# Float32 products for the last rows of gate and up weights in a mixture-of-experts trunk

## The chip, the cores and the metric

The kernel runs on one core of a Trainium2 chip. The metric is the device time of one execution in microseconds (us). Before the change it is 1541.08 us, the median of three runs (1535.46 to 1543.49).

## The reference

The reference is a trunk of two decoder layers over 256 tokens of width 1024, all in float32. Each layer projects the tokens, runs differential attention (4 heads) and a gated delta rule (4 heads) side by side, projects back, and normalises. The first layer then has a dense SwiGLU, the second a mixture of 8 experts of which each token takes 2:

```python
def swiglu(x, w_gate, w_up, w_down):
    return (jax.nn.silu(x @ w_gate) * (x @ w_up)) @ w_down
...
logits = jnp.einsum('td,de->te', xf, router_w).astype(jnp.float32)
top_val, top_idx = lax.top_k(logits, TOP_K)
gates = jax.nn.softmax(top_val, axis=-1)
...
y = swiglu(xb, w_gate[e_b], w_up[e_b], w_down[e_b])
out = jax.ops.segment_sum(y * w_buf[:, None], tok_buf, num_segments=T)
```

An expert has a gate and an up matrix of 1024 x 3584 and a down matrix of 3584 x 1024. The weights of the eight experts are 352 MB, read once. They take about 960 of the 1544 us; this is the part that the change touches, together with the first loads of the kernel.

## The kernel before, in words

**Precision.** TensorE multiplies a reduced float32 type (float32r) here. A weight piece `raw` is therefore split in two: ScalarE writes `wh`, the piece rounded to float32r (line 173), and VectorE writes `wl = raw - wh` (line 176). The activations are split the same way into a high and a low part, and the product is made of xh·wh, xl·wh and xh·wl.

**Experts.** Expert 0 comes first, then the other seven, which the kernel orders by how many tokens they drew. The three with the fewest tokens are *narrow*: they have 64 token slots. The other five are *wide*, with 128. The order is wide, narrow, wide, narrow, wide, narrow, wide, wide. An expert's hidden width is cut in two chunks of 1792 columns, numbered c = 0 and 1. For each chunk the kernel streams, in this order:

1. the gate weights in 8 pieces (k = 0 to 7) of 128 x 1792, each one DMA of 896 KB, each cut into two halves of 896 columns that are split into `wh` and `wl`; the products go to four banks of PSUM, two named `mm` and two named `gd`, 448 columns each;
2. three pieces of the down weights of the chunk before (`more()`, two rows of blocks of 1024 columns, 1 MB, two halves); the silu of the gate (`hh`, line 1165) is between the first and the second of them;
3. the up weights in 8 pieces, into four fresh banks with the same names;
4. the four pieces of down weights that remain; behind the first of them VectorE multiplies silu and up (`hh`, line 1185).

The products of a half in a wide expert are 4 with `wh` and 2 with `wl`. In a narrow expert the high and the low part of the 64 tokens lie beside each other in one stationary operand of 128 columns, so a half needs 2 products with `wh` and 2 with `wl`, and the results of the low part come out in rows 64 to 127 of the bank. At the end of a stream `leads` copies these rows to a tile `room` on ScalarE (line 1101), and four more products with a shift matrix (`moves`) add them to rows 0 to 63. `leads` is called behind the eighth piece, ahead of the first down piece; the moves come behind that down piece. `room` has two buffers, so the third and the fourth copy wait for the first two moves.

**What sets the order.** Each engine runs its instructions in an order that is fixed when the kernel is compiled. A planner makes it from the order in which the code names the instructions and from its own estimates of when each is ready; it may put an instruction ahead of an earlier one. `pin(...)` holds an instruction behind the one that was named before it on its engine, while later ones may still pass it. The copies of `leads`, the silus and the multiplications are pinned. Loads of weights are pinned on the queue of SyncE (SP), each waiting until its buffer is free: 12 buffers for raw pieces, four each for `wh` and `wl`. A buffer of a raw piece is free when VectorE has made `wl` from it.

**Start.** SP issues the positions (`pos_i`), the first constants (`cst0`), the first 128 tokens, two weight pieces of 520 KB, the other 128 tokens, two more pieces, and then the rest. Meanwhile POOL issues nine small loads, most of which broadcast a row to 128 partitions: the parameters of the delta rule (`al`), of two norms (`nrm`), of lambda (`prow`) and the router's weights (`rw`).

Of the kernel before, what the change touches and what calls it, by code (L numbers as in the profile page):

```python
# [9 lines left out]
F32 = mybir.dt.float32  # L10
# [7 lines left out]
P = 128  # L18
# [49 lines left out]
def trunk(ctx, tc, x, positions, w_in, conv_w, a_log, dt_bias, gdn_norm_w, lam_q1, lam_k1, lam_q2, lam_k2,  # L68
# [13 lines left out]
    def nm(s):  # L82
        cnt[0] += 1
        return f"{s}_{cnt[0]}"
# [118 lines left out]

    zab0 = []
    pos_i = pre.tile([P, NB], I32, name="pos_i")
    nc.sync.dma_start(pos_i, positions.rearrange("o (b p) -> p (o b)", p=P))
    nc.sync.dma_start(cst0, const[:, :P + 32])
# [768 lines left out]
    def experts(xs, jobs, mp, ring2, rest, first):  # L976
# [22 lines left out]
        def dispatch(group, early=False):  # L999
# [20 lines left out]

            return xgs, [lambda k=k: part(k) for k in range(KD)]

        def transposed(n):
            Dt = mp.tile([P, NB, P], F32R, tag="ys", name=nm("D"))
            slots(Dt, jobs[n], True)
            DT = mp.tile([P, NB, P], F32R, tag=f"DT{n % 2}", name=nm("DT"), bufs=1)
            pt = bank("a")
            for b in range(NB):
                PE.transpose(pt[:, b * P:(b + 1) * P], Dt[:, b].bitcast(F32), ident)
            V.tensor_copy(DT.rearrange("p b t -> p (b t)"), pt[:, 0:NB * P])  # L1030
            return DT

        def in_pieces(w, c, k0=0):

            for k in range(k0, KD):
                yield k, piece(w[:, k:k + 1, c * CHUNK:(c + 1) * CHUNK], 1, CHUNK)

        def products(outs, xg, narrow, k, parts):
# [56 lines left out]
        def leads(banks):  # L1095

            hi = slice(64, P)
            moves = []
            for p in banks:
                o = mp.tile([P, BANK], F32R, tag="room", name=nm("room"), bufs=2)  # L1100
                pin(S.activation(o[hi], p[hi, :], AF.Copy))
                moves.append(lambda o=o, p=p: mm(p[0:64, :], shift[hi, 0:64], o[hi], False, True))
            return moves

        def to_features(hh, narrow):
# [29 lines left out]
        for n, job in enumerate(jobs):  # L1135
            narrow = job[3]
            rows = slice(0, 64) if narrow else slice(0, P)
            xg = xgs.pop(n)
            wg, wu = (weights(n, i).rearrange("(k p) c -> p k c", p=P) for i in range(2))
            for c in range(NC):  # L1140
                banks = gu_banks()
                for k, f in enumerate(first or ()):
                    products(banks, xg, narrow, k, f)
                for sub in in_pieces(wg, c, len(first or ())):
                    products(banks, xg, narrow, *sub)
                    if side:
                        side.pop(0)()
                first = None
# [24 lines left out]
                for sub in in_pieces(wu, c):  # L1173
                    products(banks, xg, narrow, *sub)
# [4 lines left out]
                moves = leads(banks) if narrow else ()  # L1179
                more()  # L1180
                for move in moves:
                    move()
                for i, p in enumerate(banks):
                    h = hh[rows, i * BANK:(i + 1) * BANK]
                    pin(V.tensor_tensor(h, h, p[rows, :], op=ALU.mult))  # L1185
# [150 lines left out]
    nc.gpsimd.dma_start(al[:, 1], dt_bias.partition_broadcast(P))  # L1336
    nrm = pre.tile([P, 2, 2, P], F32, name="nrm")
    nc.gpsimd.dma_start(nrm[:, 0], subln_w.partition_broadcast(P))
    nc.gpsimd.dma_start(nrm[:, 1], gdn_norm_w.partition_broadcast(P))
    prow = pre.tile([P, 2 * 4 * 64], F32, name="prow")  # L1340
    for i, a in enumerate((lam_q1, lam_k1, lam_q2, lam_k2)):
        nc.gpsimd.dma_start(prow[:, i * 128:(i + 1) * 128], a.rearrange("l d -> (l d)").partition_broadcast(P))


    cw = pre.tile([P, 12, 8], F32, name="cw")


    rw = cpool.tile([P, KD, NE], F32, name="rw")
    nc.gpsimd.dma_start(rw, router_w[0].rearrange("(k p) e -> p k e", p=P))
# [72 lines left out]
```

## Time and profile before

| What | Value |
|---|---|
| median of three runs | 1541.08 us (1535.46 to 1543.49) |
| the profiled execution, its own time | 1546.4 us |
| its span on the core | 1544.4 us |
| instructions | 24332 |
| read from memory | 431.17 MB, 280 GB/s over the span |
| granted TensorE clock, mean | 0.973 of 2.4 GHz |

The span is what the profiler recorded on the core; the execution's own time is 2.0 us longer. The trace names engines PE (TensorE products), PEld (its weight loads), DVE (VectorE), ACT (ScalarE), POOL (GpSimd) and SP (SyncE's queue). A tile stands as out<-in. Products of TensorE overlap each other in the records, so their starts tell their pace, not their durations. The idle time of an engine before an instruction stands in brackets with what ended it.

### The profile page before, as it was taken

To read this page: it belongs to the slowest core of one execution; us is meant where nothing else is said; L and a number is where in the kernel's file an instruction comes from. 1 tells how busy PE (TensorE), PEld (TensorE's weight loads), DVE (VectorE), ACT (ScalarE), POOL (GpSimd) and SP (SyncE) were. 2 spreads that over 40 slices of the span, in tenths; PEclk is the share of its full clock that TensorE was granted. 3 is DMA by queue.
4 is the path that set the end of the run, shared out by engine and by line. 5 is a ranking of instruction groups with operands and counts; after the bars stand their busy time and mean duration, and the time that the engine had idled before them with its cause. 6 is when DMAs were issued, how large, how long until landed. Compare 5 with 4: busy or idle time off the path is not lost. (4 is left out here: it accounts for less than half of the span.)

```text
span 1544.4 us, 24332 instructions
## 1 busy us (share of the span) xinstructions
PE 1471.1 (95%) x8864; PEld 1239.8 (80%) x8864; DVE 1253.9 (81%) x1630; ACT 1092.3 (71%) x1577; POOL 23.6 (2%) x36
## 2 busy tenths in 40 slices
PE   7989999999999999999999999899999899999996
PEld 7968899998978888866787876688876677898884
DVE  5787655556796789888899888889889989988996
ACT  3747544456657388887787797887887878778774
POOL 1000000000000000000000000000000000000000
PEclk8999999999999799999999999999999999999998
DMA  9523465545533589999999999999999999999870
GB/s 315 208 83 110 154 203 190 191 138 188 172 109 114 191 313 367 337 394 326 366 398 330 375 358 326 379 368 351 381 339 373 330 365 400 342 356 361 306 299 31
DMA packets 89127, 433.95 MB, mean 281 GB/s; under 512 B 7816, under 2 KB 9992, under 8 KB 74912
## 3 DMA queue, kind: packets, MB, share of 16 engines
q1 hardware_dynamic: 87808, 428.54, 75.2%
q0 software_dynamic: 1184, 3.71, 0.9%
q8 instruction: 73, 1.20, 0.3%
q14 instruction: 62, 0.51, 0.1%
HBM read 431.17 MB, written 1.05 MB: 280 GB/s over the span
## 5 line engine op out<-in xcount | busy, mean ns | idle before, releaser
L176 DVE TENSOR_TENSOR wl<-raw,wh 128x896 fp32r<-128x896 f32 (+2 forms) x875 | 962.1, 1142 | 192.5 <-ACT wh L173 175.0
L173 ACT ACTIVATE wh<-raw 128x896 fp32r<-128x896 f32 (+2 forms) x875 | 844.9, 995 | 242.2 <-PE ps_gd L101 89.5
L101 PE MATMUL ps_b<-wh,hT 128*128 128x512 f32 x816 | 239.1, 405 | 7.6 <-ACT wh L173 6.0
L101 PE MATMUL ps_gd<-wh,xg 128*128 128x448 f32 x832 | 223.7, 367 | 0.0
L101 PE MATMUL ps_mm<-wh,xg 128*128 128x448 f32 x832 | 218.8, 371 | 1.0 <-ACT hh L1165 1.0
L101 PEld LDWEIGHTS ps_b<-wh,hT 128*128 128x128 f32 x816 | 155.5, 193 | 49.8 <-ACT wh L173 14.0
L101 PE MATMUL ps_b<-wl,hT 128*128 128x512 f32 x492 | 168.8, 424 | 11.2 <-DVE wl L176 11.1
L101 PEld LDWEIGHTS ps_gd<-wh,xg 128*128 128x128 f32 x832 | 156.4, 188 | 13.9
L101 PEld LDWEIGHTS ps_mm<-wh,xg 128*128 128x128 f32 x832 | 152.6, 189 | 15.3 <-ACT hh L1165 1.3
L101 PE MATMUL ps_gd<-wl,xg 128*128 128x448 f32 x512 | 153.5, 380 | 4.8 <-DVE wl L176 1.2
L101 PE MATMUL ps_mm<-wl,xg 128*128 128x448 f32 x512 | 151.1, 373 | 3.3 <-DVE wl L176 3.0
L101 PEld LDWEIGHTS ps_b<-wl,hT 128*128 128x128 f32 x492 | 91.8, 198 | 52.5 <-DVE wl L176 30.9
L101 PEld LDWEIGHTS ps_gd<-wl,xg 128*128 128x128 f32 x512 | 90.3, 188 | 34.3 <-DVE wl L176 26.1
L101 PEld LDWEIGHTS ps_mm<-wl,xg 128*128 128x128 f32 x512 | 93.3, 188 | 20.0 <-DVE wl L176 12.1
L101 PE MATMUL ps_mm<-xT,wh 128*128 128x256 f32 x448 | 70.9, 280 | 0.0
L101 PEld LDWEIGHTS ps_mm<-xT,wh 128*128 128x128 f32 x448 | 60.8, 189 | 0.4
L101 PE MATMUL ps_gd<-xT,wh 128*128 128x256 f32 x320 | 50.5, 280 | 0.0
L101 PE MATMUL ps_mm<-xT,wl 128*128 128x256 f32 x224 | 44.7, 280 | 0.0
L1119 ACT ACTIVATE hT<-ps_a 128x512 fp32r<-128x512 f32 (+2 forms) x52 | 27.5, 540 | 22.1 <-PE ps_a L1117 15.2
L101 PEld LDWEIGHTS ps_gd<-xT,wh 128*128 128x128 f32 x320 | 43.1, 189 | 0.0
L1117 PEld LDWEIGHTS ps_a<-cst,hh 128*128 128x128 f32 (+1 forms) x224 | 32.2, 201 | 6.9 <-DVE hh L1185 4.1
L1120 DVE TENSOR_TENSOR hT<-ps_a,hT 128x512 fp32r<-128x512 f32 (+2 forms) x52 | 31.8, 619 | 7.0 <-ACT hT L1119 6.9
(401 smaller groups left out, 1591.1 us busy)
## 6 DMA issues: line engine op xcount, KB each, us to landing
raw<-in_moe_w_gate_dram SPq DMA_DIRECT2D x128, 896.0 KB, 7.3
raw<-in_moe_w_up_dram SPq DMA_DIRECT2D x128, 896.0 KB, 6.5
raw<-in_moe_w_down_dram SPq DMA_DIRECT2D x110, 1024.0 KB, 6.8
raw<-in_w_in_dram SPq DMA_DIRECT2D x24, 1024.0 KB, 6.0
raw<-in_ffn_w_gate_dram SPq DMA_DIRECT2D x11, 1024.0 KB, 5.2
raw<-in_ffn_w_up_dram SPq DMA_DIRECT2D x11, 1024.0 KB, 5.1
raw<-in_ffn_w_down_dram SPq DMA_DIRECT2D x11, 1024.0 KB, 4.9
raw<-in_w_out_dram SPq DMA_DIRECT2D x8, 1024.0 KB, 4.9
```

The lines of the kernel that those rows point to most:

```text
L101: return PE.matmul(o, lhsT, rhs, start=start, stop=stop, skip_group_check=True)
L173: high = S.activation(wh[:, c:c + n], w, AF.Copy)
L176: low = V.tensor_tensor(wl[:, c:c + n], w, wh[:, c:c + n].bitcast(F32), op=ALU.subtract)
L1117: PE.transpose(pt[:, f * w:(f + 1) * w], hv[:, f0 + f], ident[rows, rows])
L1119: S.activation(hT[:, f0:f0 + n_, 0], pv, AF.Copy)
L1120: V.tensor_tensor(hT[:, f0:f0 + n_, 1], pv, hT[:, f0:f0 + n_, 0].bitcast(F32), op=ALU.subtract)
```

## The change

There are four edits.

- In a narrow expert the eighth piece (k = 7) of gate and up is loaded but not split. VectorE adds the high and the low part of the tokens once per expert into a float32 tile `x32` of 64 columns (`as_one`), and TensorE multiplies it by the raw piece in float32: four products of 448 columns in place of eight in float32r. They write rows 0 to 63.
- `leads` is called between the seventh and the eighth piece, and its four copies go to one tile of four places that shares its buffer with a wide expert's tokens (`xg`), in place of the two buffers of `room`.
- The silus (all experts) and the multiplications move behind the second down piece; the moves stay behind the first.
- At the start `cst0` is loaded ahead of `pos_i`. POOL's small loads are pinned behind a new copy on POOL that reads the last of the first four weight pieces, and so wait until it has landed.

```diff
-    nc.sync.dma_start(pos_i, positions.rearrange("o (b p) -> p (o b)", p=P))
     nc.sync.dma_start(cst0, const[:, :P + 32])
+    nc.sync.dma_start(pos_i, positions.rearrange("o (b p) -> p (o b)", p=P))
...
+        def as_one(xg):
+            x_ = mp.tile([P, 64], F32, tag="xg32", name=nm("xg32"), bufs=2)
+            V.tensor_tensor(x_, xg[:, KD - 1, 0].bitcast(F32), xg[:, KD - 1, 1].bitcast(F32), op=ALU.add)
+            return x_
...
             for k in range(k0, KD):
-                yield k, piece(w[:, k:k + 1, c * CHUNK:(c + 1) * CHUNK], 1, CHUNK)
+                src = w[:, k:k + 1, c * CHUNK:(c + 1) * CHUNK]
+                yield k, load(src, 1, CHUNK)[0] if narrow and k == KD - 1 else piece(src, 1, CHUNK)
...
+            if narrow and k == KD - 1:
+                for i, o in enumerate(outs):
+                    mm(o[0:64], x32, parts[:, i * BANK:(i + 1) * BANK], False, False)
+                return
...
-            for p in banks:
-                o = mp.tile([P, BANK], F32R, tag="room", name=nm("room"), bufs=2)
-                pin(S.activation(o[hi], p[hi, :], AF.Copy))
+            room = mp.tile([P, 4, BANK], F32R, tag=f"xg{(xg_turn[0] + 1) % 2}", name=nm("room"), bufs=1)
+            for i, p in enumerate(banks):
+                pin(S.activation(room[hi, i], p[hi, :], AF.Copy))
...
-                for sub in in_pieces(wg, c, len(first or ())):
-                    products(banks, xg, narrow, *sub)
+                moves = ()
+                for sub in in_pieces(wg, c, len(first or ()), narrow):
+                    if narrow and sub[0] == KD - 1:
+                        moves = leads(banks)
+                    products(banks, xg, narrow, *sub, x32)
...
-                moves = leads(banks) if narrow else ()
                 more()
                 for move in moves:
                     move()
+                more()
                 for i, p in enumerate(banks):
                     pin(S.activation(hh[rows, i * BANK:(i + 1) * BANK], p[rows, :], AF.Silu))
-                more()
                 more()
...
-    nc.gpsimd.dma_start(al[:, 0], a_log.partition_broadcast(P))
+    pin(G.tensor_copy(al[:, 0, 0], zab0[1][1][1][0][:, 0:4]))
+    pin(nc.gpsimd.dma_start(al[:, 0], a_log.partition_broadcast(P)))
```

The up stream is changed as the gate stream is, and the other small loads are pinned like the first.

## Rows read from the trace of the kernel before

**Rows 1.** page, part 1: engine busy us (share of span) x instructions

```profile
PE 1471.1 (95%) x8864; PEld 1239.8 (80%) x8864; DVE 1253.9 (81%) x1630; ACT 1092.3 (71%) x1577; POOL 23.6 (2%) x36
```

**Rows 2.** waits, SP's queue, 600 to 1500 us: waiter <- releaser, us, times, longest

```profile
SPq L158 <- DVE wl L176: 692.2, 330, 5.5
```

**Rows 3.** windows (us, busy, clock, DMA, GB/s): narrow expert, wide expert

```profile
882.90:1006.90 124.00, 113.57 (x470) 82.40 (x469) 109.29 (x116) 99.90 (x124) 0.00 (x0) 0.96 0.95 357
...
1006.90:1128.80 121.90, 120.67 (x578) 103.57 (x577) 111.07 (x116) 98.49 (x124) 0.00 (x0) 1.00 0.95 362
```

**Rows 4.** timeline (start, us, instructions, [idle before]), VectorE, a narrow expert

```profile
896.17 6.09 DVE L176 TENSOR_TENSOR wl<-raw,wh 128x896 fp32r<-128x896 f32 x6
903.90 1.23 DVE L176 TENSOR_TENSOR wl<-raw,wh 128x1024 fp32r<-128x1024 f32 x1 [1.65 <-ACT wh L173]
905.98 1.22 DVE L176 TENSOR_TENSOR wl<-raw,wh 128x1024 fp32r<-128x1024 f32 x1 [0.85 <-ACT wh L173]
908.77 20.67 DVE L176 TENSOR_TENSOR wl<-raw,wh 128x1024 fp32r<-128x1024 f32 x20 [1.56 <-ACT wh L173]
931.29 1.23 DVE L176 TENSOR_TENSOR wl<-raw,wh 128x1024 fp32r<-128x1024 f32 x1 [1.86 <-ACT wh L173]
933.37 1.23 DVE L176 TENSOR_TENSOR wl<-raw,wh 128x1024 fp32r<-128x1024 f32 x1 [0.85 <-ACT wh L173]
...
968.33 1.22 DVE L176 TENSOR_TENSOR wl<-raw,wh 128x1024 fp32r<-128x1024 f32 x1 [0.52 <-ACT wh L173]
972.11 20.66 DVE L176 TENSOR_TENSOR wl<-raw,wh 128x1024 fp32r<-128x1024 f32 x20 [2.56 <-ACT wh L173]
```

**Rows 5.** timeline, ScalarE, end of the first gate stream

```profile
901.82 0.97 ACT L1101 ACTIVATE room<-ps_mm 64x448 fp32r<-64x448 f32 x2 [2.49 <-PE ps_mm L101]
...
903.89 0.97 ACT L1101 ACTIVATE room<-ps_gd 64x448 fp32r<-64x448 f32 x2
...
905.97 0.97 ACT L1165 ACTIVATE hh<-ps_mm 64x448 f32<-64x448 f32 x2
```

**Rows 6.** timeline, TensorE: gate products of a narrow, down products of a wide expert

```profile
891.29 0.57 PE L101 MATMUL ps_gd<-wh,xg 128*128 128x448 f32 x2
891.69 0.57 PE L101 MATMUL ps_gd<-wl,xg 128*128 128x448 f32 x2
...
910.62 1.10 PE L101 MATMUL ps_b<-wh,hT 128*128 128x512 f32 x4
911.55 0.63 PE L101 MATMUL ps_b<-wl,hT 128*128 128x512 f32 x2
```

**Rows 7.** timeline, weight loads, float32 products 512 wide near the end of the span

```profile
1524.39 0.19 PEld L101 LDWEIGHTS ps_a<-ys,gs 128*128 128x128 f32 x1 [0.24 <-issue]
1524.82 0.19 PEld L101 LDWEIGHTS ps_a<-ys,gs 128*128 128x128 f32 x1 [0.24 <-issue]
```

**Rows 8.** windows: the stretch behind the first up stream

```profile
929.50:934.60 5.10, 4.65 (x16) 2.45 (x16) 2.45 (x3) 5.03 (x8) 0.00 (x0) 1.00 1.01 415
```

**Rows 9.** windows: a stretch of the same expert near its end

```profile
1000.80:1007.60 6.80, 6.80 (x23) 5.46 (x23) 6.80 (x7) 3.22 (x4) 0.00 (x0) 0.50 0.90 338
```

**Rows 10.** DMA queues, 0 to 21 us: packets, MB, share of 16 engines

```profile
q1 hardware_dynamic: 2438, 4.78, 67.2%
q0 software_dynamic: 320, 0.57, 20.8%
```

**Rows 11.** timeline, TensorE, 0 to 32 us

```profile
16.75 0.90 PE L233 MATMUL ps_mm<-cst,x_in 128*128 128x128 f32 x3 [4.29 <-DMA x_in<-in_x_dram]
```

**Rows 12.** timeline, ScalarE, 0 to 26 us

```profile
20.11 2.02 ACT L173 ACTIVATE wh<-raw 128x1040 fp32r<-128x1040 f32 x2
...
23.45 0.20 ACT L304 ACTIVATE nea<-al 128x4 f32<-128x4 f32 x1
23.87 2.01 ACT L173 ACTIVATE wh<-raw 128x1024 fp32r<-128x1024 f32 x2 [0.22 <-DMA raw<-in_w_in_dram]
```

**Rows 13.** tile view of the rule parameters al, its last line

```profile
DMA to landing us min/median/max: 3.8/4.4/5.0
```

More of the change, by code (lines that the diff above doesn't have):

```diff
@@ L205, in trunk @@
     pos_i = pre.tile([P, NB], I32, name="pos_i")
+    nc.sync.dma_start(cst0, const[:, :P + 32])
     nc.sync.dma_start(pos_i, positions.rearrange("o (b p) -> p (o b)", p=P))
-    nc.sync.dma_start(cst0, const[:, :P + 32])
     for b in range(NB):
@@ L1031, in transposed, with in_pieces, products @@
             return DT
-        def in_pieces(w, c, k0=0):
+        def in_pieces(w, c, k0=0, narrow=False):
             for k in range(k0, KD):
-                yield k, piece(w[:, k:k + 1, c * CHUNK:(c + 1) * CHUNK], 1, CHUNK)
-        def products(outs, xg, narrow, k, parts):
+                src = w[:, k:k + 1, c * CHUNK:(c + 1) * CHUNK]
+                yield k, load(src, 1, CHUNK)[0] if narrow and k == KD - 1 else piece(src, 1, CHUNK)
+        def products(outs, xg, narrow, k, parts, x32=None):
+            if narrow and k == KD - 1:
+                for i, o in enumerate(outs):
+                    mm(o[0:64], x32, parts[:, i * BANK:(i + 1) * BANK], False, False)
+                return
             for i, (_, wh, wl) in enumerate(parts):
@@ L1098, in leads @@
             moves = []
-            for p in banks:
-                o = mp.tile([P, BANK], F32R, tag="room", name=nm("room"), bufs=2)
-                pin(S.activation(o[hi], p[hi, :], AF.Copy))
-                moves.append(lambda o=o, p=p: mm(p[0:64, :], shift[hi, 0:64], o[hi], False, True))
+            room = mp.tile([P, 4, BANK], F32R, tag=f"xg{(xg_turn[0] + 1) % 2}", name=nm("room"), bufs=1)
+            for i, p in enumerate(banks):
+                pin(S.activation(room[hi, i], p[hi, :], AF.Copy))
+                moves.append(lambda o=room[hi, i], p=p: mm(p[0:64, :], shift[hi, 0:64], o, False, True))
             return moves
@@ L1138, in experts @@
             xg = xgs.pop(n)
+            x32 = as_one(xg) if narrow else None
             wg, wu = (weights(n, i).rearrange("(k p) c -> p k c", p=P) for i in range(2))
@@ L1172, in experts @@
                     xgs.update(zip(group, tiles))
-                for sub in in_pieces(wu, c):
-                    products(banks, xg, narrow, *sub)
+                moves = ()
+                for sub in in_pieces(wu, c, 0, narrow):
+                    if narrow and sub[0] == KD - 1:
+                        moves = leads(banks)
+                    products(banks, xg, narrow, *sub, x32)
                     if side:
@@ L1178, in experts @@
                     side.pop(0)()
-                moves = leads(banks) if narrow else ()
                 more()
@@ L1182, in experts @@
                     move()
+                more()
                 for i, p in enumerate(banks):
@@ L1334, in trunk @@
     al = pre.tile([P, 2, 2, 4], F32, name="al")
[L1335 to L1336 removed]
+    pin(G.tensor_copy(al[:, 0, 0], zab0[1][1][1][0][:, 0:4]))
+    pin(nc.gpsimd.dma_start(al[:, 0], a_log.partition_broadcast(P)))
+    pin(nc.gpsimd.dma_start(al[:, 1], dt_bias.partition_broadcast(P)))
     nrm = pre.tile([P, 2, 2, P], F32, name="nrm")
[L1338 to L1339 removed]
+    pin(nc.gpsimd.dma_start(nrm[:, 0], subln_w.partition_broadcast(P)))
+    pin(nc.gpsimd.dma_start(nrm[:, 1], gdn_norm_w.partition_broadcast(P)))
     prow = pre.tile([P, 2 * 4 * 64], F32, name="prow")
     for i, a in enumerate((lam_q1, lam_k1, lam_q2, lam_k2)):
[L1342 removed]
+        pin(nc.gpsimd.dma_start(prow[:, i * 128:(i + 1) * 128], a.rearrange("l d -> (l d)").partition_broadcast(P)))
     cw = pre.tile([P, 12, 8], F32, name="cw")
     rw = cpool.tile([P, KD, NE], F32, name="rw")
[L1349 removed]
+    pin(nc.gpsimd.dma_start(rw, router_w[0].rearrange("(k p) e -> p k e", p=P)))
     rank_r = cpool.tile([P, P], F32R, name="rank_r")
```

## The prediction

> **What bounds the kernel now.** I read the page first. It gives TensorE 95% busy [rows 1], which would say that nothing done for the other two engines can help. The records of products overlap, though, so I looked for their pace. In a narrow expert two products of a `gd` bank start 0.40 us before the next two [rows 6]: one product of 448 columns takes 0.20 us, and the four of a half take 0.81. In the same expert VectorE splits six halves in 6.09 us without a pause, 1.015 us each, and later 20 halves in 20.67 [rows 4]. So in a narrow expert's gate and up streams VectorE sets the pace, and TensorE has a fifth of its time free. The stage view says the same from the other side: TensorE is busy 120.67 of 121.90 us in a wide expert but 113.57 of 124.00 in a narrow one [rows 3]. The reader is to see that a narrow expert, with fewer products, takes no less time than a wide one.
>
> The queue of SP spends 692 of 900 us waiting for VectorE to free a raw buffer [rows 2]. Weights therefore wait in the buffers, and memory is not the limit as the kernel stands.
>
> VectorE's pauses in a narrow expert all lie where a stream ends [rows 4]. The first gate has 1.65 + 0.85 + 1.56 = 4.06 us, an up stream 1.86 + 0.85 = 2.71 (the second up has the same two), the second gate 0.52 + 2.56 = 3.08. Each time VectorE waits for a cast of ScalarE, and ScalarE is at the copies and silus [rows 5].
>
> **The splits that go.** Three narrow experts, two chunks, gate and up, two halves of the eighth piece: 24 splits of 1.015 us are gone from the engine that sets the pace, 24.4 us. ScalarE loses as many casts, and it was not the last. `as_one` adds three small operations on VectorE. Each handles 64 columns where a split handles 896; no row shows one, so they cost between nothing and three splits, 3.0 us, and I take 0.6.
>
> **The float32 products.** At the end of the span, float32 products of 512 columns load weights every 0.43 us, and each product shows up as two [rows 7]. For 448 columns that is 2 x 0.43 x 448/512 = 0.75 us, four of them 3.0 us, in place of eight products of 0.20, 1.6 us. TensorE gets 1.4 us more per stream, 16.6 us over twelve streams. I cost this at nothing, for it falls into the pause at the end of the stream, which follows. If that cover is gone it costs all 16.6.
>
> **The ends of the streams.** Let T be the time at which VectorE finishes the last split of a stream; in rows 4 the first gate has it at 896.17 + 6.09 = 902.26. The `mm` copies start at T - 0.44 [rows 5], two take 0.97, so one follows the other by 0.44. TensorE still has the last `gd` products to do, until about T + 0.7. In the new kernel all four copies have a place to go, so the `gd` copies run from T + 0.65 to T + 1.6. A down cast of 1.0 us (two take 2.01 in rows 12) follows, and VectorE restarts at about T + 2.65. That is an up stream's pause of today (2.71): no gain and no loss. TensorE runs the float32 products from T + 0.7 to T + 3.7, and the first down half is split by T + 3.8. The products are just covered.
>
> Behind a gate come the silus, now behind two down pieces. VectorE has four halves to split first at 1.11 us (what is left of 20.67 for four of 1024 columns), until T + 7.1. TensorE does two down halves of six products at 0.23 us [rows 6], held by VectorE, until T + 6.4, and the moves until T + 7.2. The first silu can start at T + 6.8. Four end at T + 8.65, and the next cast is there at T + 9.7. VectorE waits 2.6 us, or 1.4 if the planner lets one cast pass the silus. Where the pending down belongs to a narrow expert, halves need four products and all of this is 0.9 us earlier. The first gate then pauses 2.65 + 2.0 = 4.65 us against 4.06, the second 2.65 + 1.1 = 3.75 against 3.08. This loses 1.25 us per expert, 3.8 in all. At best the planner puts casts ahead of the copies everywhere and 10 us come back; at worst every silu wait is the long one and another 3.6 are lost.
>
> In the wide experts the silus' new place costs nothing: TensorE works through three down pieces before it needs the banks, and with 1.2 us of idle time per expert [rows 3] there is little to gain. I take 0, between -2 and +3.
>
> The raw buffer of the eighth piece is freed by TensorE at T + 3.7, where VectorE freed it two splits after T. The load behind it in SP's queue is issued some 2 us later, with a dozen buffers ahead of it. I take 0.
>
> On the copies "meanwhile" the Trainium skill speaks against the edit. By "PSUM — Partial Sum Buffer", section "PSUM bank collisions raise a hardware error", PSUM is to be guarded by bank and group of 32 rows, or more simply by bank. Guarded by bank, a float32 product waits for the copy of its own bank though they touch different rows. No row of before shows such a pair. What it would cost here stands under the rivals.
>
> **The start.** TensorE waits 4.29 us for the second 128 tokens, until 16.75 [rows 11]. In the first 21 us POOL's small loads hold 20.8% of the DMA engines' time for 0.57 MB, while the large loads hold 67.2% for 4.78 MB [rows 10]. Without them the tokens and the first pieces land up to 0.208 x 21 = 4.4 us earlier. I take 3.5, since part of that time lies behind them. The other end is -1: `al` lands 3.8 to 5.0 us after its issue [rows 13], POOL will now issue it at about 14 to 16, and ScalarE reads it at 23.45 today (some 20 then), ahead of casts that wait for a weight piece anyway [rows 12]. Queued behind the new copy on POOL are nine loads and two clears, all for later stages. `cst0` ahead of `pos_i` moves a load of 1 KB: nothing.
>
> **The sum.** 24.4 - 0.6 - 3.8 + 3.5 = 23.5 us. The profiled execution took 1546.4 us, which makes 1522.9; it stands 5.3 us above the median of the runs shown, and from 1541.1 the forecast is 1517.6 us.
>
> **Rivals.**
>
> *TensorE comes late at the ends.* The float32 products are not covered, because the casts for the down pieces come sooner than I think or TensorE enters the stream's end with work behind. Then 16.6 us are lost, and 6.9 of the gain remain: 1534.2. For it: the cover is 0.1 us wide. Against it: TensorE is free for a fifth of each stream.
>
> *The slower clock meets the float32 products.* The granted clock falls to 0.50, 1.2 GHz, in 6.8 us near the end of the narrow expert [rows 9], and is 0.96 on average there [rows 3], while a wide expert has 1.00. At 1.2 GHz the four products take 6.0 us. With the cover gone (6.9 left), each stream at the low clock takes 3.0 more, so from the third such stream the kernel is slower than before, and with the six of the second chunks it takes 1552.2. Against it: the products fill the very pause in which TensorE idles now.
>
> *Memory becomes the bound.* 124.0 us at 357 GB/s are 44.3 MB per narrow expert. If no more than a wide expert's 362 GB/s can be had, it cannot go below 122.3: 1.7 x 3 + 3.5 gives 1532.5. For it: DMA shares of 0.95. Against it: 415 GB/s over 5 us [rows 8], and SP waits for buffers. My forecast needs 44.3 MB in 117 us, 379.
>
> *The copies don't overlap.* If the planner lets a cast in between the pairs of copies, as now (the second pair starts 2.07 us after the first in rows 5), the `gd` copies end at T + 2.6, and a product held by its bank waits 0.4 us, twelve times: 1522.5. This is the rule of the Trainium skill cited above, "PSUM — Partial Sum Buffer", at work.
>
> *More is gained.* Casts go ahead of the copies, and each end saves 0.8 us: 1508.
>
> **How the numbers follow.** I give the forecast 0.54, late products 0.13, the slower clock 0.06, memory 0.09, no overlap 0.06, more gain 0.12. The likeliest case alone spans 1510 to 1527. The range of 1503 to 1536 leaves out the slower clock and the tails. A change under 0.5%, 7.7 us, can't be told from none. Faster by more holds in the forecast, with more gain, without overlap, and in about half of the memory case and a third of the late one: 0.81. Slower is the clock case, 0.06. The rest is 0.13.
>
> **What would show it.** Right: VectorE splits 14 halves of 896 columns per narrow stream at 1.0 us; a narrow expert takes 116 to 118 us; its pauses are near 2.65 us behind an up stream and 4 behind a gate; the second tokens are multiplied at about 13 us. Wrong: VectorE waits in the middle of a narrow stream, or for TensorE; the float32 starts lie more than 0.38 us apart; ScalarE waits for weights; a wide expert takes more than 122 us.

## The result, and the profile after

The changed kernel takes 1522.83 us (median of 4 runs, 1522.21 to 1524.3) against 1542.28 us for the kernel before on the same chip (1535.46 to 1545.24). The ratio is 0.9881, 95% interval 0.9847 to 0.9916: 19.4 us less. The profiled execution of after took 1522.21 us (span 1520.1), that of before 1546.4 (span 1544.4) and so about 4 us more than its median. Between the two profiles there are thus 24.3 us to explain.

The page's part 1 and SP's waits of after, 600 to 1500 us, answer to [rows 1, 2]:

```profile
PE 1466.2 (96%) x8864; PEld 1227.9 (81%) x8864; DVE 1228.5 (81%) x1609; ACT 1068.5 (70%) x1553; POOL 23.8 (2%) x37
```

```profile
SPq L158 <- DVE wl L176: 618.4, 310, 5.3
SPq L158 <- PE ps_mm L101: 24.8, 6, 4.1
```

VectorE has 25.4 us less to do; 24 splits of 1.015 us less three `as_one` of 0.22 make 23.7 of it. SP still waits for buffers, so memory did not become the bound.

By stage, in windows of after (narrow expert, then the wide one behind it), the same columns as [rows 3]:

```profile
869.20:989.40 120.20, 114.52 (x474) 78.89 (x473) 100.78 (x107) 92.75 (x117) 0.00 (x0) 1.00 0.97 366
989.40:1109.20 119.80, 117.94 (x573) 102.65 (x572) 111.32 (x118) 97.67 (x124) 0.00 (x0) 1.00 0.96 369
```

From VectorE's first gate split of an expert to that of the next, the narrow expert takes 120.2 us instead of 123.9, while VectorE's work in it fell by 8.5. So 4.8 us of what was taken from VectorE came back as waiting. The wide expert, whose arithmetic is the same, takes 119.8 instead of 122.0.

The waiting is in VectorE's timeline of this narrow expert, which answers to [rows 4]:

```profile
869.06 0.22 DVE L1026 TENSOR_TENSOR xg<-xg 128x64 f32<-128x64 f32 x1
...
881.78 4.09 DVE L176 TENSOR_TENSOR wl<-raw,wh 128x896 fp32r<-128x896 f32 x4
889.51 4.63 DVE L176 TENSOR_TENSOR wl<-raw,wh 128x1024 fp32r<-128x1024 f32 x4 [3.64 <-ACT wh L173]
896.16 16.39 DVE L176 TENSOR_TENSOR wl<-raw,wh 128x1024 fp32r<-128x1024 f32 x16 [2.02 <-ACT wh L173]
916.42 4.63 DVE L176 TENSOR_TENSOR wl<-raw,wh 128x1024 fp32r<-128x1024 f32 x4 [3.87 <-ACT wh L173]
...
952.23 4.63 DVE L176 TENSOR_TENSOR wl<-raw,wh 128x1024 fp32r<-128x1024 f32 x4 [3.64 <-ACT wh L173]
957.95 16.39 DVE L176 TENSOR_TENSOR wl<-raw,wh 128x1024 fp32r<-128x1024 f32 x16 [1.09 <-ACT wh L173]
978.20 4.63 DVE L176 TENSOR_TENSOR wl<-raw,wh 128x1024 fp32r<-128x1024 f32 x4 [3.86 <-ACT wh L173]
```

The pauses are 5.66 + 3.87 + 4.73 + 3.86 = 18.1 us per narrow expert. Before they were 4.06 + 2.71 + 3.08 + 2.71 = 12.6 [rows 4].

Why they grew stands in ScalarE's and TensorE's timelines at the end of the first gate (ScalarE's answers to [rows 5]):

```profile
885.43 0.97 ACT L1115 ACTIVATE room<-ps_mm 64x448 fp32r<-64x448 f32 x2 [2.67 <-PE ps_mm L101]
887.43 0.97 ACT L1115 ACTIVATE room<-ps_gd 64x448 fp32r<-64x448 f32 x2 [1.03 <-PE ps_gd L101]
888.42 3.90 ACT L173 ACTIVATE wh<-raw 128x1024 fp32r<-128x1024 f32 x4
```

```profile
884.93 0.68 PE L101 MATMUL ps_mm<-wl,xg 128*128 128x448 f32 x2
886.02 0.97 PE L101 MATMUL ps_mm<-raw,xg 128*64 128x448 f32 x2 [0.42 <-ACT room L1115]
886.92 0.67 PE L101 MATMUL ps_gd<-wl,xg 128*128 128x448 f32 x2
887.52 0.96 PE L101 MATMUL ps_mm<-raw,xg 128*64 128x448 f32 x2
888.32 1.67 PE L101 MATMUL ps_gd<-raw,xg 128*64 128x448 f32 x4
```

The planner put the first float32 product (written in two records, `ps_mm<-raw`) ahead of the last two `gd` products (`ps_gd<-wl`). That product waits 0.42 us for the copy of its own bank, and the `gd` products behind it in TensorE's queue wait with it. ScalarE then waits 1.03 us for `gd`, the down casts stand behind ScalarE's copies, and VectorE behind the casts. It is so in 11 of the 12 narrow streams. The four float32 products take 3.3 us of TensorE (0.90 + 0.80 + 1.60 from start to start) and end 0.4 us behind VectorE's pause, when the first down half is still being split.

The start. DMA queues of after, 0 to 21 us, TensorE at the second row block, and ScalarE at the rule's parameters answer to [rows 10 to 12]:

```profile
q1 hardware_dynamic: 3137, 6.16, 84.8%
q0 software_dynamic: 220, 0.41, 7.1%
```

```profile
10.49 0.85 PE L233 MATMUL ps_mm<-cst,x_in 128*128 128x128 f32 x3
```

```profile
18.57 0.21 ACT L304 ACTIVATE nea<-al 128x4 f32<-128x4 f32 x1 [1.85 <-DMA al<-in_a_log_dram]
```

The second 128 tokens are multiplied at 10.49 us instead of 16.75, 6.3 us sooner. The tile view of x has the landing of its two loads, counted from their issue, before and then after:

```profile
DMA to landing us min/median/max: 5.0/9.3/13.5
```

```profile
DMA to landing us min/median/max: 3.5/5.0/6.4
```

The shortest is the first load and the longest the second: 5.0 and 13.5 us before, 3.5 and 6.4 after. The first product of the main projection begins at 23.66 where it began at 31.22, 7.6 us sooner, and 8.5 us are still won at 510 us. So the 1.85 us for which the late `al` holds ScalarE delay nothing that lasts.

The clock. Windows of after at the end of the narrow expert (answering to [rows 9]) and of the one narrow expert at whose end the clock still falls:

```profile
982.50:989.30 6.80, 6.15 (x33) 4.94 (x33) 6.80 (x9) 4.22 (x5) 0.00 (x0) 1.00 1.00 396
...
1227.40:1230.80 3.40, 3.40 (x9) 2.65 (x8) 3.40 (x4) 0.95 (x1) 0.00 (x0) 0.51 0.98 349
```

Where before had 6.8 us at 1.2 GHz at the end of the narrow expert, after has 2.4 GHz. In the 6.8 us ahead of the fall TensorE of before was busy for 5.22; in the 6.8 us ahead of 982.5 in after it was busy throughout, with the float32 products and what follows them. TensorE then enters the wide expert with less work left over: its first gate product of the wide expert starts 2.9 us behind VectorE's first split in before (1009.73), and 0.7 in after (990.11). Over the whole span TensorE stood at 1.2 GHz for 82 us in before and 50 us in after; between 560 and 1485 us, most of the experts' part, it was 31 and 10.

So the 24.3 us are: 8.5 by 510 us, 10.2 in the three narrow experts (2.76, 3.72, 3.71), 5.0 in the three wide ones behind them (2.06, 2.21, 0.78), and 0.6 elsewhere.

### The profile page after: what moved, and what is told of

Read it like the earlier page. It is cut to its first block, busy times and chain, and to the rows that moved or that the text cites. A ratio compares the mean times of both kernels' runs of the same rounds, so it can differ in the third digit from the quotient of the medians.

```text
span 1520.1 us, 24270 instructions
## 1 busy us (share of the span) xinstructions
PE 1466.2 (96%) x8864; PEld 1227.9 (81%) x8864; DVE 1228.5 (81%) x1609; ACT 1068.5 (70%) x1553; POOL 23.8 (2%) x37
## 3 DMA queue, kind: packets, MB, share of 16 engines
q0 software_dynamic: 1184, 3.71, 0.8%
## 4 chain that ended last, share of the span: by engine, by line
PE 79%; DVE 9%; ACT 5%; DMA 4%; issue 2%; SPq 0%; DVEq 0%; ACTq 0%
PE ps_mm L101 23%; PE ps_gd L101 23%; PE ps_b L101 22%; PE ps_a L101 9%; DVE wl L176 6%; ACT wh L173 2%; DMA raw<-in_moe_w_up_dram 2%; DMA raw<-in_moe_w_down_dram 2%; PE ps_a L1131 2%; ACT hh L1183 1%; DVE hh L1205 0%; ACT room L1115 0%; DVE x_in L1095 0%; PE ps_mm L562 0%; DVE hT L1134 0%
## 5 line engine op out<-in xcount | busy, mean ns | idle before, releaser
L176 DVE TENSOR_TENSOR wl<-raw,wh 128x896 fp32r<-128x896 f32 (+2 forms) x851 | 938.8, 1144 | 199.3 <-ACT wh L173 182.6
L173 ACT ACTIVATE wh<-raw 128x896 fp32r<-128x896 f32 (+2 forms) x851 | 822.2, 997 | 236.3 <-PE ps_gd L101 91.1
L101 PE MATMUL ps_b<-wh,hT 128*128 128x512 f32 x816 | 233.7, 398 | 0.7 <-ACT hT L1133 0.7
L101 PE MATMUL ps_gd<-wh,xg 128*128 128x448 f32 x808 | 217.0, 368 | 0.0
L101 PE MATMUL ps_mm<-wh,xg 128*128 128x448 f32 x808 | 214.0, 372 | 1.0 <-ACT hh L1183 1.0
L101 PE MATMUL ps_b<-wl,hT 128*128 128x512 f32 x492 | 159.0, 403 | 5.8 <-DVE wl L176 5.8
L101 PEld LDWEIGHTS ps_gd<-wh,xg 128*128 128x128 f32 x808 | 152.5, 189 | 13.5
L101 PEld LDWEIGHTS ps_mm<-wh,xg 128*128 128x128 f32 x808 | 148.7, 190 | 15.3 <-ACT hh L1183 1.3
L101 PE MATMUL ps_gd<-wl,xg 128*128 128x448 f32 x488 | 146.6, 381 | 4.4 <-DVE wl L176 0.8
L101 PE MATMUL ps_mm<-wl,xg 128*128 128x448 f32 x488 | 144.7, 374 | 2.0 <-DVE wl L176 1.5
```

The costliest lines, as they stand in the source:

```text
L101: return PE.matmul(o, lhsT, rhs, start=start, stop=stop, skip_group_check=True)
L173: high = S.activation(wh[:, c:c + n], w, AF.Copy)
L176: low = V.tensor_tensor(wl[:, c:c + n], w, wh[:, c:c + n].bitcast(F32), op=ALU.subtract)
```

## The experiments

The ratios are to the kernel before, measured on the same chip. Experts are named n0 to n7 in order; n1, n3 and n5 are narrow. An expert's time is from its first gate split to the next expert's, in the one execution that was profiled. Gains in us are worked out from the ratio, or from the two medians where that is said; the two ways differ by up to 2 us.

**1. The start alone** (before with the two edits ahead of layer 0):

```
+    nc.sync.dma_start(cst0, ...)          # ahead of pos_i
+    pin(G.tensor_copy(al[:, 0, 0], zab0[1][1][1][0][:, 0:4]))
+    pin(nc.gpsimd.dma_start(al[:, 0], ...))   # and the loads behind it
```

> Only the edits at the start are made. Two accounts of the 19 us. (a) The start is worth more than the sum gave it: in the two traces the first product of the main projection is 7.6 us earlier and the layers after it 8.4 us. Then this kernel takes about 8.4 us less than before, a ratio near 0.9945. (b) The start is worth the 3.5 us of the sum and the rest of the shift comes from the clock of the two executions that happened to be profiled: then the ratio is near 0.998.

Measured: 1536.31 us, ratio 0.9956 (0.9939 to 0.9973), 6.8 us, or 4.2 to 9.4 by the interval. The start is worth about twice the 3.5 us of my sum. That it is more than the sum's upper bound of 4.4 is likely and not certain.

**2. Everything but the start** (after with those edits undone):

```
-    pin(G.tensor_copy(al[:, 0, 0], ...))
...
```

> All edits but those at the start. If the parts add up, the 19.4 us of the whole less the 8.4 of (a) leave 11 us (ratio 0.993 to before); under (b) some 16 us (0.990). The narrow experts' own account in the two traces is 10.2 us, and 4.8 us more in the wide experts that follow them.

Measured: 1530.64 us, 0.9922 (0.9906 to 0.9937), 11.9 us between the medians. The start and the rest add within the noise: 6.8 + 11.9 = 18.7 beside 19.4.

**3. The first float32 product held back** (after; it is pinned behind the last split-weight product):

```
-                    mm(o[0:64], x32, parts[...], False, False)
+                    ins = mm(o[0:64], x32, parts[...], False, False)
+                    if i == 0:
+                        pin(ins)
```

> The changed kernel with the first float32 product of a stream pinned behind the last float32r product. In 11 of 12 streams the planner has put it ahead of the last two gd products; it waits 0.42 us for the copy of its bank and takes 0.75 more, and the gd copies and all that ScalarE does behind them come about 1.0 us later than in the sum. If that is why VectorE restarts 3.64 to 3.87 us after a stream and not 2.65, the pause falls to about 2.7 and the kernel takes some 11 us less than the changed one (near 1512). Rival: the pause is set by the casts' place behind four copies and by nothing TensorE does; then the time stays within 2 us of the changed kernel's.

Measured: 1516.61 us, 0.9836 (0.9818 to 0.9854), 6.2 us below after's median where I had expected some 11. VectorE and TensorE at the end of the first gate of n3:

```profile
876.05 4.09 DVE L176 TENSOR_TENSOR wl<-raw,wh 128x896 fp32r<-128x896 f32 x4
882.78 3.50 DVE L176 TENSOR_TENSOR wl<-raw,wh 128x1024 fp32r<-128x1024 f32 x3 [2.64 <-ACT wh L173]
```

```profile
880.19 0.67 PE L101 MATMUL ps_gd<-wl,xg 128*128 128x448 f32 x2 [0.33 <-DVE wl L176]
880.79 1.72 PE L101 MATMUL ps_mm<-raw,xg 128*64 128x448 f32 x4
```

The pause is 2.64 us here and 2.65 to 2.73 in the other three streams, the T + 2.65 of my sum. So the order of two products on TensorE, and nothing slower, made 3.64 to 3.87 of it. n3 takes 118.1 us, 2.1 less than in after and not the 4 us of four shorter pauses. Behind a gate VectorE pauses a second time, for the casts behind the silus, and these pauses grew: 2.77 and 1.84 us where after has 2.02 and 1.09. All pauses of n3 behind its streams are now 2.64 + 2.77 + 2.73 + 2.65 + 1.84 + 2.72 = 15.3 us.

**4. The casts ahead of the copies** (after; the first down piece is named ahead of `leads`, its products stay where they were):

```
                     if narrow and sub[0] == KD - 1:
+                        ahead.append(next(downs))
                         moves = leads(banks)
```

> The changed kernel with the first down piece of each narrow stream named ahead of the four copies, so that its two casts stand in front of them on ScalarE, in the time in which it now waits 2.7 us for TensorE. If VectorE's pause behind a stream is the price of those copies, it goes (3.6 to 3.9 us, twelve times, less up to 1.5 us that come back at the silus): 25 to 40 us less than the changed kernel, 1483 to 1498. Rival: the float32 products lose their cover, TensorE becomes the last engine in the narrow experts (16.6 us of added products show) and the gain is 10 to 20 us. Third: memory can't give 44.3 MB in less than about 115 us per narrow expert, ScalarE then waits for weights, and the gain stops at 15 us.

Measured: 1507.6 us, 0.9771 (0.9751 to 0.9792), 15.2 us below after's median. That is far from the 25 to 40 of the first account and within the 10 to 20 of the rival. VectorE in n3, windows of n3 and n4, and ScalarE's longest wait in n3, here and then in after (us, times, longest):

```profile
876.79 6.36 DVE L176 TENSOR_TENSOR wl<-raw,wh 128x896 fp32r<-128x896 f32 x6
883.53 2.36 DVE L176 TENSOR_TENSOR wl<-raw,wh 128x1024 fp32r<-128x1024 f32 x2 [0.38 <-ACT wh L173]
886.44 1.23 DVE L176 TENSOR_TENSOR wl<-raw,wh 128x1024 fp32r<-128x1024 f32 x1 [0.56 <-issue]
888.41 1.22 DVE L176 TENSOR_TENSOR wl<-raw,wh 128x1024 fp32r<-128x1024 f32 x1 [0.74 <-ACT wh L173]
891.10 2.23 DVE L176 TENSOR_TENSOR wl<-raw,wh 128x896 fp32r<-128x896 f32 x2 [1.47 <-ACT wh L173]
```

```profile
864.20:977.30 113.10, 110.13 (x463) 78.25 (x462) 101.73 (x107) 92.92 (x117) 0.00 (x0) 1.00 0.97 381
977.30:1099.60 122.30, 120.44 (x584) 104.50 (x584) 111.69 (x119) 97.59 (x124) 0.00 (x0) 1.00 0.96 370
```

```profile
ACT wh L173 <- PE ps_b L101: 10.2, 16, 1.9
...
ACT wh L173 <- PE ps_b L101: 4.2, 9, 0.9
```

A pause of 5.66 us in two pieces became 3.15 in four, and TensorE has work in each. n3 falls to 113.1 us, with TensorE busy for 110.1 of it. Behind a stream's end TensorE is now the last: ScalarE's casts wait for its down products to free the buffers of `wh`, 10.2 us in n3 instead of 4.2. 2.5 us of the 7.1 come back in the wide expert behind (122.3 instead of 119.8), for TensorE's first gate product there starts 2.2 us behind VectorE's first split, in after 0.7. The third account is out: memory gave n3 381 GB/s, and no cast of n3 waited for a weight. What the float32 products cost without their cover was not measured by itself.

**5, 6. The two halves of the start** (before with the later loads of GpSimd's queue alone; before with the order of SyncE's two loads alone):

```
+    pin(G.tensor_copy(al[:, 0, 0], zab0[1][1][1][0][:, 0:4]))     # 5
+    pin(nc.gpsimd.dma_start(al[:, 0], ...))
```

```
+    nc.sync.dma_start(cst0, const[:, :P + 32])                    # 6
     nc.sync.dma_start(pos_i, ...)
-    nc.sync.dma_start(cst0, const[:, :P + 32])
```

> The kernel before with one half of the start edits: the small broadcast loads of GpSimd's queue wait for the second row block of x; the order of SyncE's first two loads stays as before. Start edits together measured a ratio of 0.9956 (6.8 us). Theory (a), the broadcast packets slow the loads of x beside them: this half has most of it, the second row block is read by TensorE at about 11 to 12 us instead of 16.75, the ratio is 0.9960 to 0.9975 (4 to 6 us). Rival (b), the gain is the identity matrix arriving ahead of the positions: this half alone gives under 1.5 us, a ratio of 0.999 or more, and the second row block still at 15 to 17 us.

> The kernel before with the other half: the identity block is loaded ahead of the positions, the loads of GpSimd's queue stay where they were. Theory (a): the first transposes begin 1.6 us sooner (6.93 to about 5.4 us), but the second row block still lands at about 16 us behind the broadcast packets, so 0 to 1.5 us in the end, a ratio of 0.999 to 1.000. Rival (b): the whole start gain, a ratio of 0.9956 to 0.997.

Measured: 1536.59 us, 0.9955 (0.9938 to 0.9972) for the loads, 1541.64 us, 0.9995 (0.9977 to 1.0012) for the order. TensorE at the second row block, first with the loads later, then with the order alone:

```profile
10.53 0.84 PE L233 MATMUL ps_mm<-cst,x_in 128*128 128x128 f32 x3
```

```profile
17.62 0.90 PE L233 MATMUL ps_mm<-cst,x_in 128*128 128x128 f32 x3 [4.94 <-DMA x_in<-in_x_dram]
```

The whole start is the small loads' place in time. The order of the two loads does nothing that can be measured, not even for the first transposes, which begin at 7.00 us (6.93 before): they wait for x.

**7. The silus alone** (before with the silus and the products of gate and up behind a second down piece, in all experts):

```
                 more()
                 for move in moves: move()
+                more()
                 for i, p in enumerate(banks):
                     pin(S.activation(hh[...], p[rows, :], AF.Silu))
```

> The kernel before with the silus and the products of up behind two down pieces and nothing else. Theory (a): in narrow experts the scheduler already puts two pieces' casts ahead of the silus, so nothing moves there; in wide ones one more piece of down work stands on TensorE before the first gate product of the next stream, which TensorE, busy 120.67 of 121.90 us, can't shorten: ratio 0.999 to 1.001. Rival (b): the 2 us that the wide experts behind a narrow one gained (6 us in all) come from this order: ratio 0.996 to 0.997, those experts at about 119.5 us.

Measured: 1534.75 us, 0.9956 (0.994 to 0.9972), 7.4 us between the medians and 6.8 by the ratio. My theory of no effect fell. VectorE behind the first gate of the wide expert n4, in before and in this kernel, and n3 and n4 of this kernel in windows:

```profile
1026.55 2.44 DVE L176 TENSOR_TENSOR wl<-raw,wh 128x1024 fp32r<-128x1024 f32 x2 [0.25 <-DMA raw<-in_moe_w_up_dram]
1031.33 7.64 DVE L176 TENSOR_TENSOR wl<-raw,wh 128x1024 fp32r<-128x1024 f32 x7 [2.34 <-ACT wh L173]
```

```profile
1016.63 4.89 DVE L176 TENSOR_TENSOR wl<-raw,wh 128x1024 fp32r<-128x1024 f32 x4 [0.25 <-ACT wh L173]
1022.97 5.37 DVE L176 TENSOR_TENSOR wl<-raw,wh 128x1024 fp32r<-128x1024 f32 x5 [1.45 <-ACT wh L173]
```

```profile
876.30:999.00 122.70, 115.45 (x475) 83.59 (x474) 109.25 (x116) 100.50 (x125) 0.00 (x0) 0.96 0.95 360
999.00:1118.70 119.70, 117.84 (x572) 102.68 (x571) 111.19 (x118) 97.60 (x124) 0.00 (x0) 1.00 0.96 369
```

With one piece ahead, VectorE stands 2.34 us behind ScalarE's four silus, and the three down pieces take it 9.41 us; with two pieces it is 1.45 and 8.70. The wide expert of before, with TensorE busy for 120.67 of 121.90 us [rows 3], had 2 us to give all the same; experiment 12 comes back to whose they were.

**8. The copies behind the float32 products** (after; nothing is copied meanwhile):

```
-                        moves = leads(banks)
                     products(banks, xg, narrow, *sub, x32)
+                    if narrow and sub[0] == KD - 1:
+                        moves = leads(banks)
```

> The changed kernel with each stream's four room copies behind the float32 products instead of ahead of them, so that the second part is not copied meanwhile. Theory (a): the copies then wait for the last float32 product (about 3 us of products), ScalarE's down casts stand behind the copies, and VectorE restarts 1 to 2.3 us later than in the changed kernel (pauses of 4.7 to 6 us instead of 3.64 and 3.87), in 12 streams 12 to 28 us: 1535 to 1550 us, a ratio of 0.995 to 1.006 to the kernel before. Rival (b), the order that the scheduler writes hides it, since the first float32 product waits for the copy of its own bank now and would not then: 0.986 to 0.991, pauses of 3 to 4 us.

Measured: 1531.16 us, 0.9929 (0.9903 to 0.9955), some 7 to 8 us above after: between the two theories, and with an interval that reaches into both. VectorE behind the first gate and the first up stream of n3:

```profile
891.94 1.23 DVE L176 TENSOR_TENSOR wl<-raw,wh 128x1024 fp32r<-128x1024 f32 x1 [2.32 <-ACT wh L173]
894.95 1.23 DVE L176 TENSOR_TENSOR wl<-raw,wh 128x1024 fp32r<-128x1024 f32 x1 [1.78 <-ACT wh L173]
...
920.82 1.23 DVE L176 TENSOR_TENSOR wl<-raw,wh 128x1024 fp32r<-128x1024 f32 x1 [4.79 <-ACT wh L173]
```

Behind an up stream the pause is the 4.7 us of (a). Behind a gate the planner lets a cast pass the copies, and it is 2.3 + 1.8. n3 takes 123.2 us, 3.0 more than in after: copying meanwhile is worth that per narrow expert.

**9. The narrow part alone** (before with float32 last rows and early copies; start and silus as before), told against after:

```
-                more()                    # ahead of the silus
                 for i, p in enumerate(banks):
                     pin(S.activation(hh[...], p[rows, :], AF.Silu))
+                more()
...
```

> The kernel before with the narrow experts' part alone: last rows in float32, the joined columns and the copies ahead of the last products; silus behind one down piece, start as before. Theory (a), the parts add: the changed kernel without its start edits has 11.9 us and the silus alone have 6.8 to 7.4, so 4.5 to 5.1 us are left for this part, a ratio of 0.9965 to 0.9975, and the wide experts (121 us) stay as they were. Rival (b), the silus' gain and this part's are the same time gained twice (both shorten the ends of narrow streams): 8 to 12 us alone, a ratio of 0.992 to 0.995.

Measured: 1536.52 us, 0.9953 (0.9935 to 0.9971), 7.2 us, between both theories too, and the interval again reaches into both. Windows of n3 and n4:

```profile
880.50:1003.30 122.80, 118.03 (x478) 81.49 (x476) 101.07 (x108) 93.21 (x117) 0.00 (x0) 0.97 0.95 358
1003.30:1123.20 119.90, 118.69 (x569) 101.88 (x569) 110.83 (x118) 97.53 (x123) 0.00 (x0) 1.00 0.96 370
```

The narrow expert wins only 1.2 us. The wide one wins 2.1 us, and its code is that of before. In this profile no stretch at 1.2 GHz lies at the end of a narrow expert. The same was seen in part with the start alone, where that stretch was 3.4 us long at the end of n3 and n4 took 120.6 us:

```profile
1000.20:1120.80 120.60, 119.38 (x573) 102.55 (x572) 111.06 (x117) 97.93 (x124) 0.00 (x0) 1.00 0.96 367
```

**10, 11. A third down piece ahead of the silus**, on top of experiment 4, in wide experts only (10), and also ahead of the products of gate and up (11):

```
                 more()
+                if not narrow:
+                    more()
                 for i, p in enumerate(banks):
```

> The changed kernel with the first down piece's casts named ahead of the copies (0.9771 before) and, in wide experts only, the silus behind a third down piece. Theory (a): the silus on ScalarE still hold up the third piece's casts (VectorE waits 1.45 us for ScalarE at the end of a wide gate with two pieces, 2.34 with one), so one piece more takes the rest of that wait and 0.4 to 0.7 us in each of some ten wide gates: 3 to 7 us, a ratio of 0.9725 to 0.9755. Rival (b): the banks that the silus free come late for the first products of up, TensorE waits 1 to 2 us at each: 0.978 to 0.984.

> The same, and also the products of gate and up behind a third down piece in wide experts. Theory (a): at the end of up these products stand on VectorE, whose splits they delay, and the transposes of the result wait for them; a third piece gives TensorE work meanwhile, 0 to 0.5 us at each of ten ends beyond the run above: 0.970 to 0.976. Rival (b): the transposes and the casts of the result for the next down products come later and those products wait, 0.5 to 1 us each: 0.977 to 0.982.

Measured: 1505.27 us, 0.9756 (0.9733 to 0.9778), and 1508.49 us, 0.9771 (0.9747 to 0.9796), beside 0.9771 without. These can't be told apart. 10 lies just beyond its theory (a) and 11 at the near edge of its rival (b), so a third piece is not shown to be worth anything. Versions 4 and 10 have the shortest times of all, 2.3 and 2.4% below the kernel before.

**12. The silus in narrow experts only** (in wide ones they stay behind one piece):

```
+                if narrow:
+                    more()
                 for i, p in enumerate(banks):
```

> The kernel before with the silus and the products of up behind two down pieces in narrow experts only; wide experts' code is that of before. The silus in all experts gave 7.4 us (0.9956), of which the wide experts behind a narrow one had 2 us each. Theory (a), the clock: what the wide experts gained is the stretch at 1.2 GHz behind the end of a narrow expert (6.8 us before, 3.4 us with the silus moved), which the narrow expert's own order shortens, so they gain the same without a change of their own: 119.6 to 120.3 us against 121.4 to 122.0, a ratio of 0.9950 to 0.9970 (4.5 to 7.5 us). Rival (b), the order in the wide experts themselves (VectorE waits 1.45 us for ScalarE at the end of a gate instead of 2.34): they stay at 121 to 122 us, and 2 to 3 us are left of the gain, a ratio of 0.998 to 0.999.

Measured: 1541.55 us, 0.9994 (0.9976 to 1.0012). Theory (a) fell: the narrow experts' own order by itself brings nothing that can be measured. So the silus' 7 us need the new order in the wide experts; that order alone was not run. In the profiles of 12 and 7 they lie in n4 (121.3 against 119.7 us), and in the narrow experts behind wide ones (123.8 against 122.6), in whose first gate the wide expert's last down pieces are worked off. How much of the wide experts' gain is the order and how much the clock can be read from TensorE. In windows from its first gate product of n4 to its first of n5, in before and then in after:

```profile
1009.73:1132.25 122.52, 121.29 (x581) 104.13 (x580) 111.87 (x117) 99.72 (x126) 0.00 (x0) 1.00 0.95 361
...
990.11:1111.95 121.84, 119.98 (x581) 104.37 (x580) 113.36 (x120) 99.56 (x126) 0.00 (x0) 1.00 0.96 368
```

Counted so, n2, n4 and n6 take 122.1, 122.5 and 122.1 us in before and, within 0.2, in every run with the old order in the wide experts (1, 5, 6, 9, 12), whatever the clock did ahead of them. With the new order they take 121.3 to 121.5, 121.8 to 121.9 and 121.2 to 121.4 (after, 2, 3, 7, 8). So the order is worth 0.6 to 0.9 us in each. The rest of the 2 us is work that the narrow expert's end left to TensorE: in 12 its first gate product of n6, with no stretch at 1.2 GHz at the end of n5, started 0.7 us behind VectorE's first split and n6 took 119.5 us by VectorE; in before 2.8 us behind, and 121.5. How the 7 us divide over the whole kernel is not settled by this, since n0, n7 and the narrow experts have their part.

## Why the prediction was right, and where it was not

The forecast of 1517.6 us is 5 us from the 1522.8 measured and the sum of 23.5 stands beside 24.3 between the profiles and 19.4 between the medians. What set the pace, VectorE's splits, was read rightly. But three of the terms were wrong and made up for each other, so that the sum came this near was luck.

*The splits that go, and `as_one`: right.* 8.5 us less of VectorE's work per narrow expert; 14 halves of 896 columns at 1.01 us each per stream; `as_one` took 0.22 us an expert.

*The float32 products: right.* In a row their records start 0.37 to 0.38 us apart, 0.75 us a product as I had it; where after breaks the row up, the four take 3.3 us of TensorE instead of 3.0. VectorE's pauses end on ScalarE's casts, not on TensorE. In experiment 4, where most of the pause behind a gate is gone, the narrow expert still got 7.1 us shorter. The rival of the late TensorE appears only there, in ScalarE's waits for TensorE and in the 2.5 us that the wide expert behind gives back.

*The ends of the streams: mis-sized, the largest error.* I let them lose 1.25 us per narrow expert; they lost 5.5 (18.1 against 12.6). The first step that failed is "the `gd` copies run from T + 0.65". Two pairs of copies did follow each other 2.00 us apart, as the rival "the copies don't overlap" had them, by way of the 0.42 us that it names: a product into rows 0 to 63 of a bank waits for the copy of its rows 64 to 127. The Trainium skill ("PSUM — Partial Sum Buffer", section "PSUM bank collisions raise a hardware error") asks for a guard by bank and group of 32 rows, or more simply by bank. By the finer guard the copies would not hold the products, which write other rows, so the skill does not speak against the edit as the prediction has it. The trace agrees with the simpler one: the product waits for its own bank, 0.42 us. No run here shows what two engines on different rows of one bank would do. What I missed is that a product that waits so can stand ahead of others that need not wait. Experiment 3 takes that away and finds my 2.65 us. I had worked out the dependences of the stream's end, and not the order that the planner would write. The second step that failed is the wait behind the silus, 2.0 and 1.1 us in my sum: with the order mended it was 2.77 and 1.84, the larger part of why experiment 3 won only half of what I expected of it. The narrow part, 20.0 in my sum, was worth 7.2 alone (4.5 to 10 by the interval). That the copies' rival, at a chance of 0.06, forecast 1522.5, all but the time measured, is luck as well, since other terms of its sum were off.

*The silus in wide experts: wrong.* "I take 0, between -2 and +3" was worth 7 us. I read 120.67 of 121.90 us busy as a bound on what could be won. Counted from TensorE's own first product, its busy time in a wide expert is 121.29 of 122.52 us in before and 119.98 of 121.84 in after, 581 products at the full clock in both. The records of the same products were 1.3 us longer in one order than in the other, so a busy TensorE is no floor. I had said so of the page and then used it of the stage. Besides, my window began at VectorE's first split, and its first 2.8 us of busy TensorE were work left over from the narrow expert.

*The start: mis-sized.* 3.5 us, at most 4.4, from the share that POOL's loads held [rows 10]; measured 6.8. By the same rows a byte of those loads held the engines 2.6 times as long as one of the large loads (20.8% for 0.57 MB, 67.2% for 4.78 MB). But the cost was not the share: the second load of x landed 13.5 us after its issue before and 6.4 after, 7.1 us sooner where the share allowed 4.4, and everything of the first layer begins with these loads. The Trainium skill ("DMA: Bandwidth & Descriptors", section "Queues, rings and completion order") has an engine take turns between its queues packet by packet. By that rule a load would wait for each slow packet beside it. The trace agrees as far as the delay goes, 1.5 us at the first load of x and 7.1 at the second; no run here shows the turns.

*The clock: a gain that I had only as a rival's loss.* With the old order in the wide experts, n2 and n6 took 121.4 to 121.6 us behind 6.8 us at 1.2 GHz at the end of the narrow expert, 120.5 to 120.8 behind 3.4 us, and 119.5 to 119.6 behind none (before and experiments 1, 5, 6, 9, 12). So each such stretch that went gave back up to 2 us. It is not the length of VectorE's pauses that decides: in experiment 9 they are longer than in before, and the stretches at the ends are gone. Between 560 and 1485 us, runs without the float32 products (before, 1, 5, 6, 7, 12) had 10 to 31 us at 1.2 GHz, and runs with them (after, 2, 3, 4, 8 to 11) 0 to 10; after and 12 both had 10. This fits what I had argued against the rival, that the products fill the pause in which TensorE idled, and does not prove it. Experiment 6, with the experts' code of before, had 3.4 us ahead of n4 and n6 and 6.8 ahead of n2, so one code can go either way.

The three parts alone add to 20.8 us by their ratios (6.8 + 6.8 + 7.2), and the whole is 18.4 by its own. A part of the time may be won by more than one of them, but the difference is within the noise.

Of the other rivals, memory was no bound: 366 GB/s in after, 381 in experiment 4, with SP still waiting for VectorE. SP waited also for TensorE to free the eighth piece's buffer, 24.8 us at the `mm` products, and nothing shows that this cost time. Of the marks that I named, those at the splits' pace and the wide expert held; 116 to 118 us for a narrow expert (120.2), pauses of 2.65 and 4 us (3.87 and 4.7 to 5.7) and the second tokens at about 13 us (10.49) did not.

## What to carry to other kernels

Where instructions of several engines meet at the end of a stage, draw the order in each engine's queue, not only the dependences: one instruction that waits 0.4 us made VectorE's pause 1 us longer at nearly every stream end because of what stood behind it, and the kernel 6 us slower. A forecast of a sum can be right with wrong terms, so run the parts alone. Work taken off the engine that sets the pace is won only if the pauses at stage ends don't grow; naming the next stage's first casts ahead of the copies (experiment 4) was worth 15 us on top of the whole change's 19. And count a stage from the engine that finishes it last: what one engine's window shows as a gain of a stage can be work that the stage before no longer leaves over.

## What the runs showed of the hardware

- Small loads of 0.57 MB on the software queue, most of them broadcasts, held 20.8% of the DMA engines' time in the first 21 us, delayed the first product on the second load of x by 6.3 us and cost the whole kernel 6.8. Issued from 13 us on, they left all of the 7.6 us won at the main projection standing at 510 us.
- Float32 products of 448 columns take two records each that start 0.37 to 0.38 us apart at 2.4 GHz, 0.75 us a product, where a float32r product takes 0.20.
- Time at 1.2 GHz at the end of a stage is paid in part in the stage behind it, by VectorE's windows about 2 us in a wide expert for 6.8 us and 1 us for 3.4, in the same code. Over the whole span the time at 1.2 GHz was 82 us in before, 50 in after, 35 in experiment 3 and 33 in experiment 4.
